# State space layer: pools allocated in another order, the next mixer's earliest weights split from inside it, and ScalarE's opening reordered

## The chip, the cores and the metric

The kernel runs on one core of one Trainium2 chip. The metric is the device time of one launch in microseconds (us), the median over several runs. A core has five engines with a queue of instructions each: PE (TensorE: matrix products and transposes), DVE (VectorE), ACT (ScalarE), POOL (GpSimd) and SP (SyncE, which here issues most of the transfers). An engine takes its instructions in the order that the compiler's scheduler wrote; semaphores tie the engines together.

## The reference

An encoder trunk of two layers over 512 tokens of 1024 numbers, in float32. Each layer is a token mixer and a channel mixer with a normalisation before and after:

```python
for layer in range(DEPTH):                       # DEPTH = 2
    hn = rms_norm(x, norm_mix_pre[layer])
    m = retention_na_mixer(hn, ...) if layer % 2 == 0 else ssd_mixer(hn, ...)
    x = x + rms_norm(m, norm_mix_post[layer])
    f = conv_geglu_ffn(rms_norm(x, norm_ffn_pre[layer]), ...)
    x = x + rms_norm(f, norm_ffn_post[layer])
```

Layer 0's mixer is retention beside neighbourhood attention. Layer 1's is a state space mixer: one projection gives gates z, inputs xs, keys B, queries C and step sizes; a depthwise convolution of width 5 and a silu follow; a scan runs in both directions in chunks of 128 tokens; `y * silu(z)` is normalised in four groups and projected back. The channel mixer projects to 2 x 2816 features, convolves over three tokens, takes `gelu(gate) * value` and projects back.

## The kernel before, in words

The program is four stages on one core: `mixer0` and `ffn` for layer 0, `mixer1` and `ffn` for layer 1, with x resident in SBUF as four tiles of 128 tokens, t0 to t3. Tokens that feed a product are normalised (`norm`: a sum of squares on ACT, `ssx`, tile junk; `r_x` by a power on POOL; `xs` in two halves on DVE), transposed by PE eight blocks at a time (`turn`, tile pt, L148), and split into a high part xh (an ACT cast, L86) and a low part xl (a DVE subtraction, L87). Products run in a reduced-precision float format, so each is three: high with high, high with low, low with high (`mm3`, L91 to L93).

Weights come from DRAM as 128 x 1024 float32 pieces, 512 KB each, into the tile wst, of which there are three; SP issues the loads in program order. `wunit` loads a piece and splits it in the same manner: an ACT cast to whi, a DVE subtraction to wlo. For some pieces the parts lie elsewhere: the third and fourth weight of an ffn are split into four half pieces, hh and hl.

A scheduler orders the instructions of each engine. It is told priorities (`high_priority(n)`), and follows dependences between tiles and those added by hand with `together`. Tiles come out of pools; a pool's place in memory depends on the order in which pools are opened, and a tile that reuses a place waits for the last user of it, so the order of pools is itself an input to the schedule.

`mixer1` handles four groups of eight heads. A table (`SLOTS`) lists in which order the steps of a group are written: `n` and `t` project the next weights (bf, cf, xf: key, query and input, each followed by ACT's first tap of the convolution, L693, and four DVE taps, L696), `h` makes a head's decay matrix (rows pb are broadcast from DRAM by a transfer that ACT issues, L751; eight ACT steps shift them, L762; a DVE copy masks them; ACT takes the exponential into `e`, L766; DVE multiplies), `i` and `p` do the products pi and py and end with y, N the silus (z, L702 and L705). Exponential and silu need different function tables, and ACT loads one (ACT_TABLE_LOAD) at each switch. The epilogue projects y back, tile by tile (m), adds it to x, which is reloaded from DRAM half by half (xd, L869), and normalises the sum (`ssm`, `r_m`, mg, x). `finish` runs these steps as they are listed in TAIL and LATE.

`ffn` begins with four projections (two features pieces, gate and value) over the first 256 tokens and then over the second 256, so that it can start before the last tokens are ready; between them E.flush() lets the last tiles' transposes in. In the products of this stage the first two weights are whi, wlo and the next two hh, hl.

At the program's start the four tiles of x are loaded, with the first three weights of `mixer0` between them, and each is normalised and turned.

## Time and profile before

| | us |
|---|---|
| median of three runs | 1422.65 |
| runs | 1420.84, 1422.65, 1425.30 |
| the profiled execution | 1422.91, its span 1421.1 |
| PE busy in the span | 1395.8 (98%) |
| DVE, ACT, POOL busy | 909.3, 710.6, 60.9 |
| PE's first transposes start | 8.17 |
| mixer1's first group of heads | from about 700 |
| start of the second ffn | about 1044 |

In the rows of the timeline the first number is the start in us from the start of the span, the second the busy time, then engine, line, operation, the tile written and those read; `x3` says how many follow on each other. In square brackets stands the idle time of the engine ahead of the row and the engine, tile and line that ended it. The profile's line numbers are those of the kernel before. A table of stretches gives, for each stretch, its length, the busy time of PE, PE's weight loads, DVE, ACT and POOL, the granted clock of PE as a share of full speed, the share of the transfer engines in use and GB/s.

### The profile page before, as it was taken

To read this page: it belongs to the slowest core of one execution; us is meant where nothing else is said; L and a number is where in the kernel's file an instruction comes from. 1 tells how busy PE (TensorE), PEld (TensorE's weight loads), DVE (VectorE), ACT (ScalarE), POOL (GpSimd) and SP (SyncE) were. 2 spreads that over 40 slices of the span, in tenths; PEclk is the share of its full clock that TensorE was granted. 3 is DMA by queue.
4 is the path that set the end of the run, shared out by engine and by line. 5 is a ranking of instruction groups with operands and counts; after the bars stand their busy time and mean duration, and the time that the engine had idled before them with its cause. 6 is when DMAs were issued, how large, how long until landed. Compare 5 with 4: busy or idle time off the path is not lost.

```text
span 1421.1 us, 17833 instructions
## 1 busy us (share of the span) xinstructions
PE 1395.8 (98%) x6838; PEld 1141.2 (80%) x6838; DVE 909.3 (64%) x1345; ACT 710.6 (50%) x1194; POOL 60.9 (4%) x66
## 2 busy tenths in 40 slices
PE   7999999999999999999999999999989999999998
PEld 6877777898888888888788788787878888888886
DVE  7368888765656652347878686997785665664232
ACT  5346666444444432324878787487344444443230
POOL 1010110100000000000000000010110000000000
PEclk9999999999999999999999999999999999999999
DMA  7443232233233322323566464363342233333231
GB/s 284 150 132 104 85 89 80 77 108 104 89 104 91 102 89 93 129 106 106 140 183 182 148 184 143 101 190 112 124 144 74 91 102 91 102 96 98 89 104 60
DMA packets 56437, 166.33 MB, mean 117 GB/s; under 512 B 6689, under 2 KB 7457, under 8 KB 56353
## 3 DMA queue, kind: packets, MB, share of 16 engines
q1 hardware_dynamic: 48464, 149.99, 33.2%
q10 hardware_dynamic: 7888, 15.21, 3.9%
q8 instruction: 54, 0.88, 0.3%
q14 instruction: 31, 0.25, 0.1%
HBM read 157.57 MB, written 5.51 MB: 115 GB/s over the span
## 4 chain that ended last, share of the span: by engine, by line
PE 89%; DVE 4%; ACT 3%; issue 2%; DMA 1%; POOL 0%; DVEq 0%; SPq 0%; POOLq 0%; ACTq 0%
PE mm L91 27%; PE mm L92 27%; PE mm L93 27%; PE pi L783 2%; PE py L803 1%; PE st L732 1%; PE y L459 1%; PE pt L148 1%; PE sc L443 1%; DVE wlo L87 1%; PE pt L676 0%; PE sc L444 0%; ACT whi L86 0%; DMA x<-in_x 0%; PE pt L511 0%
## 5 line engine op out<-in xcount | busy, mean ns | idle before, releaser
L91 PE MATMUL mm<-xh,whi 128*128 128x512 f32 (+1 forms) x1216 | 463.9, 382 | 0.4 <-ACT xh L86 0.2
L93 PE MATMUL mm<-xl,whi 128*128 128x512 f32 (+2 forms) x1216 | 463.3, 381 | 0.0
L92 PE MATMUL mm<-xh,wlo 128*128 128x512 f32 (+2 forms) x1216 | 462.1, 380 | 0.0
L87 DVE TENSOR_TENSOR wlo<-wst,whi 128x1024 fp32r<-128x1024 f32 (+1 forms) x208 | 254.8, 1226 | 135.0 <-ACT whi L86 131.7
L86 ACT CAST whi<-wst 128x1024 fp32r<-128x1024 f32 (+1 forms) x208 | 216.5, 1042 | 145.1 <-PE mm L92 123.4
L91 PEld LDWEIGHTS mm<-xh,whi 128*128 128x128 f32 x1216 | 228.3, 188 | 45.7 <-issue 2.3
L93 PEld LDWEIGHTS mm<-xl,whi 128*128 128x128 f32 (+1 forms) x1216 | 228.1, 188 | 44.1 <-issue 1.1
L92 PEld LDWEIGHTS mm<-xh,wlo 128*128 128x128 f32 (+1 forms) x1216 | 228.4, 188 | 42.4 <-issue 0.2
L237 DVE SCALAR_TENSOR_TENSOR cv<-mm,cwt,cv 128x511 f32<-128x511 f32 x88 | 66.0, 750 | 150.5 <-ACT cv L236 150.5
L236 ACT ACTIVATE cv<-mm,cwt 128x512 f32<-128x512 f32 x88 | 68.7, 780 | 128.0 <-PE mm L93 128.0
L91 PE MATMUL mm<-whi,hh 128*128 128x512 f32 x288 | 112.0, 389 | 0.0
L92 PE MATMUL mm<-whi,hl 128*128 128x512 f32 x288 | 112.0, 389 | 0.0
L93 PE MATMUL mm<-wlo,hh 128*128 128x512 f32 x288 | 112.0, 389 | 0.0
L762 ACT ACTIVATE pb<-pb,tok 128x128 f32<-128x128 f32 x256 | 81.3, 391 | 5.7 <-DMA pb<-pd 3.2
L86 ACT CAST hh<-cv 128x512 fp32r<-128x512 f32 x44 | 27.3, 621 | 103.3 <-DVE cv L245 103.3
L238 DVE SCALAR_TENSOR_TENSOR cv<-mm,cwt,cv 128x511 f32<-128x511 f32 x88 | 66.0, 750 | 3.0
L93 PEld LDWEIGHTS mm<-wlo,hh 128*128 128x128 f32 x288 | 54.1, 188 | 11.3
L91 PEld LDWEIGHTS mm<-whi,hh 128*128 128x128 f32 x288 | 54.1, 188 | 11.2
L92 PEld LDWEIGHTS mm<-whi,hl 128*128 128x128 f32 x288 | 54.1, 188 | 11.2
L696 DVE SCALAR_TENSOR_TENSOR xf<-mm,cwt,xf 128x511 f32<-128x511 f32 (+1 forms) x64 | 47.5, 744 | 8.1 <-ACT xf L693 7.8
L87 DVE TENSOR_TENSOR hl<-cv,hh 128x512 fp32r<-128x512 f32 x44 | 30.5, 693 | 28.9 <-ACT hh L86 28.9
L128 ACT ACTIVATE junk<-mm 128x512 bf16<-128x512 f32 x24 | 14.3, 596 | 68.7 <-PE mm L93 68.6
(250 smaller groups left out, 1877.1 us busy)
## 6 DMA issues: line engine op xcount, KB each, us to landing
wst<-in_f_up SPq DMA_DIRECT2D x88, 512.0 KB
wst<-in_f_down SPq DMA_DIRECT2D x44, 512.0 KB
wst<-in_c_fm SPq DMA_DIRECT2D x40, 512.0 KB
pb<-pd ACTq DMA_DIRECT2D x29, 512.0 KB
wst<-in_ab_fm SPq DMA_DIRECT2D x20, 512.0 KB
gain<-yd SPq DMA_DIRECT2D x32, 256.0 KB
wst<-in_c_out SPq DMA_DIRECT2D x16, 512.0 KB
gain<-in_norms SPq DMA_DIRECT2D x8, 512.0 KB
```

The costliest lines, as they stand in the source:

```text
L86: self.nc.scalar.copy(hi, src)
L87: self.nc.vector.tensor_tensor(lo, src, hi.bitcast(F32), op=ALU.subtract)
L91: mm(out, lh, rh, start=first, stop=False)
L92: mm(out, ll, rh, start=False, stop=False)
L93: mm(out, lh, rl, start=False, stop=last)
L128: self.nc.scalar.activation(self.junk[:, :w], src, AF.Square, scale=float(n) ** -0.5, accum_out=s)
L236: nc.scalar.activation(o, ps, AF.Identity, scale=w(1), bias=w(3))
L237: nc.vector.scalar_tensor_tensor(o[:, 1:], ps[:, :S - 1], w(0), o[:, 1:], op0=ALU.mult, op1=ALU.add)
L238: nc.vector.scalar_tensor_tensor(o[:, :S - 1], ps[:, 1:], w(2), o[:, :S - 1], op0=ALU.mult, op1=ALU.add)
L696: nc.vector.scalar_tensor_tensor(r[:, a], ps[:, b], wc(j), r[:, a], op0=ALU.mult, op1=ALU.add)
L762: nc.scalar.activation(pb[:, dr, c], pb[:, dr, c], AF.Identity, scale=1.0 - 2 * dr, bias=tok[:, 0, c, dr * H + h:dr * H + h + 1])
L783: nc.tensor.matmul(pi[:, c - 1 + dr], o["st"][dr, i][:, q * P:(q + 1) * P], o["t"][1][:, c * C:(c + 1) * C], start=True, stop=True)
```

## The change

It has three parts, and none changes what is computed. The instructions are the same but for one ACT instruction more.

In the opening, ACT gets a square of a single number ahead of everything else, which brings its table. The loads of `mixer0`'s first weights stay where they were, and their splits are written behind the turning of the tokens: a weight's cast is tied behind the second xh cast of tile t, and the square of t1 behind the first xh cast of t0.

In `mixer1` the pools ys and last are opened ahead of `three`, and the rows pb leave `three` for a pool of their own, hrows, with three buffers. The small tiles ss and rg go to another pool, a gap of 32 numbers and a smaller pad keep the addresses of others, and the epilogue's mg comes from `three` under the tag e, in place of z's place.

Between `mixer1` and the second `ffn`, `ahead` loads and splits the ffn's first two weights from inside `mixer1`, the second behind the last yh, and loads the third. In `ffn` the splits of the third and fourth weight (hh) are tied behind the last xh cast of t1, those of the fifth and sixth behind the last xh cast of t2 and t3.


```diff
@@ Env
-        pool("pad", 1).tile([P, 80], F32, name="pad")
+        pool("pad", 1).tile([P, 48], F32, name="pad")
...
-        self.late, self.xs = [], {}
-
-    def wunit(self, src, parts=None):
-
-
-        nc = self.nc
+        self.late, self.xs, self.turned = [], {}, {}
+
+    def wload(self, src):
+
         st = self.wst.tile([P, 1024], F32, name="wst")
-        nc.sync.dma_start(st, src)
+        self.nc.sync.dma_start(st, src)
+        return st
+
+    def wunit(self, src, parts=None, st=None, ahead=60, behind=None):
+        if st is None:
+            st = self.wload(src)
...
-            with self.tc.high_priority(60):
-                self.split(hi, lo, st)
+            with self.tc.high_priority(ahead) if ahead else nullcontext():
+                self.split(hi, lo, st, behind)
...
-    def split(self, hi, lo, src):
-
-        self.nc.scalar.copy(hi, src)
+    def split(self, hi, lo, src, behind=None):
+
+
+        first = self.nc.scalar.copy(hi, src)
         self.nc.vector.tensor_tensor(lo, src, hi.bitcast(F32), op=ALU.subtract)
+        if behind:
+            self.together([first], [behind])
+        return first
...
-    def norm(self, t, g_pre):
+    def norm(self, t, g_pre, behind=None):
 
         nc = self.nc
-        r = self.power("x", self.sumsq(self.xe[:, t, :], D, "ssx"))
+        r = self.power("x", self.sumsq(self.xe[:, t, :], D, "ssx", behind))
...
-                self.split(self.xh[o], self.xl[o], pt)
+                self.turned.setdefault(t, [None, None])[h] = self.split(self.xh[o], self.xl[o], pt)
@@ ffn
-def ffn(E, w_up, cw, w_down, g_post_row, done):
+def ffn(E, w_up, cw, w_down, g_post_row, done, w1=None):
...
-        nc.sync.dma_start(cwt, cw)
...
-        w0 = [[E.wunit(w_up[s, f], extra() if 2 * f + s >= 2 else None) for s in range(2)] for f in range(2)]
+        u0, u1, st = w1 or (E.wunit(w_up[0, 0]), E.wunit(w_up[1, 0]), None)
+
+        behind = E.turned[1][1] if w1 else None
+        w0 = [[u0, u1], [E.wunit(w_up[0, 1], extra(), st, behind=behind), E.wunit(w_up[1, 1], extra(), behind=behind)]]
+        nc.sync.dma_start(cwt, cw)
...
-                w = E.wunit(w_up[s, f])
+                w = E.wunit(w_up[s, f], behind=E.turned[2 + s][1] if w1 and f == 2 else None)
@@ mixer1
-def mixer1(E, w_dt, w_fm, cw, dtc, cols, mask, w_out, g_post_row, done):
+def mixer1(E, w_dt, w_fm, cw, dtc, cols, mask, w_out, g_post_row, done, ahead):
...
+        few.tile([P, 32], F32, name="gap")
         few.tile([P, 32], F32, name="pad")
...
-                pbs.append(three.tile([P, 2, NT, C], F32, name="pb", bufs=3))
+                pbs.append(hrows.tile([P, 2, NT, C], F32, name="pb"))
...
-            nc.scalar.activation(yh, y, AF.Identity, scale=col[:, 1, f:f + 1])
+            o["yh"] = nc.scalar.activation(yh, y, AF.Identity, scale=col[:, 1, f:f + 1])
...
-            o["ss"] = few.tile([P, NT], F32, name="ss", bufs=2)
+            o["ss"] = E.small.tile([P, NT], F32, name="ss", bufs=2)
...
-            o["r"] = few.tile([P, NT], F32, name="rg", bufs=2)
+            o["r"] = E.small.tile([P, NT], F32, name="rg", bufs=2)
...
-        three, ys, last = pool("m1e", 5), pool("m1y", 2), pool("m1f", 1)
+        ys, last, hrows, three = pool("m1y", 2), pool("m1f", 1), pool("m1p", 3), pool("m1e", 5)
...
-            E.post_half(st, t, n, m, g_post, None, four.tile([P, 512], F32, name="mg", tag="z"))
+            E.post_half(st, t, n, m, g_post, None, three.tile([P, 512], F32, name="mg", tag="e"))
...
+        ahead(gs[-1]["yh"])
         first = [out_mm(gs[-1], 0, ws[n]) for n in range(2)]
@@ trunk
-        w0 = []
+        ws, w0 = [], []
...
                 g0 = E.bcast(norms[0, 0])
+
+                nc.scalar.activation(E.junk[:, :1], E.mhalf, AF.Square)
             else:
-                w0.append(E.wunit(ab[0][0, len(w0)]))
+                ws.append(E.wload(ab[0][0, len(ws)]))
         for t in range(NT):
-            E.norm(t, g0)
+
+            E.norm(t, g0, E.turned[0][0] if t == 1 else None)
             E.turn(t, 0 if t else 100)
+            if t < len(ws):
+                w0.append(E.wunit(None, st=ws[t], ahead=0, behind=E.turned[t][1]))
...
-        mixer1(E, *ssd, norms[1, 1], then(norms[1, 2]))
-        ffn(E, *ffns[1], norms[1, 3], store)
+        w1 = []
+
+        def ahead(w):
+            up = ffns[1][0]
+            w1.extend((E.wunit(up[0, 0]), E.wunit(up[1, 0], behind=w), E.wload(up[0, 1])))
+
+        mixer1(E, *ssd, norms[1, 1], then(norms[1, 2]), ahead)
+        ffn(E, *ffns[1], norms[1, 3], store, w1)
```

The order on the engines moves more than these lines say. On ACT, in the first group of `mixer1`, before (whi_6056 is the cast of the weight for cf):

```order
L762 ACTIVATE pb_5493<-pb_5493,tok_5147 128x128 x8
L86 CAST whi_6056<-wst_6054 128x1024
L766 ACT_TABLE_LOAD
L766 ACTIVATE e_5783<-pb_5489 128x512
L766 ACTIVATE e_5865<-pb_5491 128x512
L751 DMA pb_5785<-pd_5149 128x2x512
L751 DMA pb_5867<-pd_5149 128x2x512
L702 ACT_TABLE_LOAD
L702 ACTIVATE z_5851<-mm_5826 128x512
L705 ACTIVATE z_5708<-mm_5683 128x512
L705 ACTIVATE z_5740<-mm_5715 128x512
L705 ACTIVATE z_5819<-mm_5794 128x512
```

and with the change (the same weight is whi_6061, bf_5942 is the first tap of the key convolution):

```order
L827 ACTIVATE sq_5886<-y_5763 128x512
L841 ACTIVATE yh_5888<-y_5763,col_5140 128x512
L780 ACTIVATE pb_5790<-pb_5790,tok_5149 128x128 x7
L780 ACTIVATE pb_5872<-pb_5872,tok_5149 128x128 x3
L784 ACT_TABLE_LOAD
L784 ACTIVATE e_5971<-pb_5790 128x512
L711 ACTIVATE bf_5942<-mm_5917,cwt_5136 128x512
L769 DMA pb_5973<-pd_5151 128x2x512
L780 ACTIVATE pb_5872<-pb_5872,tok_5149 128x128 x2
L93 CAST whi_6061<-wst_6059 128x1024
L780 ACTIVATE pb_5872<-pb_5872,tok_5149 128x128 x3
L93 CAST whi_6112<-wst_6110 128x1024
```

The cast of this weight stood ahead of the first exponentials; it now stands behind y's square, ten steps of pb, a table load, an exponential and bf.

On ACT, at the start of the second ffn, before (pt_8995 and pt_9002 are the transposes of tile t2; hh are the third and fourth weight, whi_9228 the sixth):

```order
L86 CAST xh_100<-pt_8995 128x4x128
L86 CAST xh_100<-pt_9002 128x4x128
L86 CAST whi_9228<-wst_9226 128x1024
L86 CAST hh_8923<-wst_8927 128x512
L86 CAST hh_8924<-wst_8927 128x512
L86 CAST hh_8933<-wst_8937 128x512
L86 CAST hh_8934<-wst_8937 128x512
L128 ACTIVATE junk_99,ssx_8874<-x_97 128x1025
```

and with the change (pt_8901 and pt_8908 are those of t1, pt_9001 and pt_9008 of t2; whi_9203 is the fifth weight; ssm1 is the last square of t3):

```order
L93 CAST xh_100<-pt_8901 128x4x128
L93 CAST xh_100<-pt_8908 128x4x128
L93 CAST hh_8930<-wst_8659 128x512
L93 CAST hh_8931<-wst_8659 128x512
L93 CAST hh_8938<-wst_8942 128x512
L93 CAST hh_8939<-wst_8942 128x512
L138 ACTIVATE junk_99,ssx_8825<-x_97 128x1025
L138 ACTIVATE junk_99,ssm0_8864<-m_8860 128x512
L93 CAST xh_100<-pt_9001 128x4x128
L93 CAST xh_100<-pt_9008 128x4x128
L93 CAST whi_9203<-wst_9201 128x1024
L138 ACTIVATE junk_99,ssm1_8884<-m_8880 128x512
```

The hh casts moved from behind t2's casts and a weight's to right behind t1's; a weight's cast now stands between t2's xh casts and the square ssm1 of t3.

On DVE at the same place, before (the last two x are tile t3's; wlo_9198 is the fifth weight's):

```order
L161 TENSOR_TENSOR mg_8844<-m_8841,gain_8608 128x512
L868 SCALAR_TENSOR_TENSOR m_8861<-mm_8848,rg_8674,x_97 128x512
L87 TENSOR_TENSOR wlo_9198<-wst_9195,whi_9197 128x1024
L139 SCALAR_TENSOR_TENSOR xs_8810<-x_97,r_x_8808,gain_8696 128x512
L139 SCALAR_TENSOR_TENSOR xs_8812<-x_97,r_x_8808,gain_8696 128x512
L114 TENSOR_SCALAR v_m_8867<-ssm0_8845,ssm1_8865 128x1
L161 TENSOR_TENSOR mg_8864<-m_8861,gain_8608 128x512
L185 SCALAR_TENSOR_TENSOR x_97<-mg_8844,r_m_8869,x_97 128x512
L185 SCALAR_TENSOR_TENSOR x_97<-mg_8864,r_m_8869,x_97 128x512
L87 TENSOR_TENSOR xl_101<-pt_8995,xh_100 128x4x128
```

and with the change (v_m is what POOL makes r_m of t3 from; x and xs are of t3):

```order
L886 SCALAR_TENSOR_TENSOR m_8880<-mm_8867,rg_8693,x_97 128x512
L94 TENSOR_TENSOR xl_101<-pt_9001,xh_100 128x4x128
L173 TENSOR_TENSOR mg_8883<-m_8880,gain_8613 128x512
L94 TENSOR_TENSOR xl_101<-pt_9008,xh_100 128x4x128
L124 TENSOR_SCALAR v_m_8886<-ssm0_8864,ssm1_8884 128x1
L94 TENSOR_TENSOR wlo_9204<-wst_9201,whi_9203 128x1024
L197 SCALAR_TENSOR_TENSOR x_97<-mg_8863,r_m_8888,x_97 128x512
L197 SCALAR_TENSOR_TENSOR x_97<-mg_8883,r_m_8888,x_97 128x512
L151 SCALAR_TENSOR_TENSOR xs_8897<-x_97,r_x_8895,gain_8715 128x512
L151 SCALAR_TENSOR_TENSOR xs_8899<-x_97,r_x_8895,gain_8715 128x512
```

The fifth weight's wlo stood ahead of t2's xs; it now stands between v_m and x of t3.

More of the change, by code (lines that the diff above doesn't have):

```diff
@@ L69, in wunit @@
             hi, lo = self.whi.tile([P, 1024], R32, name="whi"), self.wlo.tile([P, 1024], R32, name="wlo")
-            with self.tc.high_priority(60):
-                self.split(hi, lo, st)
+            with self.tc.high_priority(ahead) if ahead else nullcontext():
+                self.split(hi, lo, st, behind)
             return [(hi[:, c], lo[:, c]) for c in halves]
-        with self.tc.high_priority(60):
+        with self.tc.high_priority(ahead):
             for j, c in enumerate(halves):
-                self.split(parts[j], parts[j + 2], st[:, c])
+                self.split(parts[j], parts[j + 2], st[:, c], behind)
         return [(parts[j], parts[j + 2]) for j in range(2)]
@@ L122, in power, with sumsq @@
         return r
-    def sumsq(self, src, n, name):
+    def sumsq(self, src, n, name, behind=None):
         s = self.small.tile([P, 1], F32, name=name)
         w = src.shape[-1]
-        self.nc.scalar.activation(self.junk[:, :w], src, AF.Square, scale=float(n) ** -0.5, accum_out=s)
+        m = self.nc.scalar.activation(self.junk[:, :w], src, AF.Square, scale=float(n) ** -0.5, accum_out=s)
+        if behind:
+            self.together([m], [behind])
         return s
-    def norm(self, t, g_pre):
+    def norm(self, t, g_pre, behind=None):
         nc = self.nc
-        r = self.power("x", self.sumsq(self.xe[:, t, :], D, "ssx"))
+        r = self.power("x", self.sumsq(self.xe[:, t, :], D, "ssx", behind))
         self.xs[t] = []
```

## The prediction, as it was made before the run

> **What bounds the kernel now.** I read the page's busy times first, then the waits of PE, then the clock and the queues at each long wait. In the waits the columns are total us, times, longest.
>
> ```profile
> PE 1395.8 (98%) x6838; PEld 1141.2 (80%) x6838; DVE 909.3 (64%) x1345; ACT 710.6 (50%) x1194; POOL 60.9 (4%) x66
> PE pt L148 <- DVE xs L139: 9.1, 4, 8.2
> PE mm L91 <- ACT hh L86: 3.9, 2, 3.2
> PE pi L783 <- DVE state L740: 0.5, 1, 0.5
> ```
>
> PE is the bound: 25.3 us of the span are idle, and only PE's waits can be won back. The edits can reach the opening (8.2), the start of the second ffn (3.9 and a slow clock behind it), and the state space mixer, where PE hardly waits and any new wait is a loss. PE's program has the same products before and after.
>
> The start of the second ffn, PE, then the clock (PEclk is the seventh figure: the share of full speed) and the queues of ACT and SP:
>
> ```profile
> 1050.91 1.29 PE L148 MATMUL pt<-head,xs 128*128 128x128 f32 x8
> 1055.42 0.38 PE L91 MATMUL mm<-xh,hh 128*128 128x256 f32 x1 [3.21 <-ACT hh L86]
> 1056.46 0.58 PE L91 MATMUL mm<-xh,hh 128*128 128x256 f32 x1 [0.66 <-ACT hh L86]
> 1062.06 1.29 PE L148 MATMUL pt<-head,xs 128*128 128x128 f32 x8
> 1065.93 0.28 PE L91 MATMUL mm<-xh,whi 128*128 128x256 f32 x1
> 1066.30 0.28 PE L91 MATMUL mm<-xh,whi 128*128 128x256 f32 x1
> ...
> 1054.00:1056.00 2.00, 0.38 (x1) 0.19 (x1) 2.00 (x3) 2.00 (x4) 0.00 (x0) 0.94 0.71 244
> 1056.00:1062.00 6.00, 5.54 (x24) 5.30 (x25) 4.15 (x7) 1.98 (x4) 1.08 (x1) 0.50 0.69 219
> 1062.00:1064.00 2.00, 2.00 (x17) 2.00 (x16) 0.43 (x1) 1.05 (x2) 0.00 (x0) 0.85 0.32 129
> ...
> 1043.89 1.25 ACT L86 CAST xh<-pt 128x512 fp32r<-128x512 f32 x2 [0.71 <-PE pt L148]
> 1051.58 1.25 ACT L86 CAST xh<-pt 128x512 fp32r<-128x512 f32 x2 [1.64 <-PE pt L148]
> 1053.80 1.04 ACT L86 CAST whi<-wst 128x1024 fp32r<-128x1024 f32 x1 [0.97 <-DMA wst<-in_f_up]
> 1054.75 2.17 ACT L86 CAST hh<-wst 128x512 fp32r<-128x512 f32 x4
> 1056.83 1.06 ACT L128 ACTIVATE junk<-x 128x1025 bf16<-128x1025 f32 x1
> ...
> 1028.84 19.95 SPq L869 DMA_DIRECT2D x<-xd  x8
> 1049.64 0.33 SPq L66 DMA_DIRECT2D wst<-in_f_up  x1
> ```
>
> PE needs hh at about 1052.2 and gets it at 1055.42. ACT was held by the cast at 1053.80, whose weight was asked for at 1049.64, behind eight reloads of x. Then the clock halves: at half speed it ran for 0.24 us of 1054-56, all 6.0 of 1056-62 and 0.60 of 1062-64, 6.8 us in all, of which PE was busy some 6.1 and lost half, 3.0. The pass over the second half of the tokens starts at 1065.93. Products of 256 columns follow each other by (1066.30 - 1065.93)/3 = 0.12 us.
>
> **The change, start of the ffn.** The four hh casts now stand right behind t1's xh casts; of the casts to whi, the fifth weight's stands behind t2's xh, the sixth's, which held them, behind t3's. In the clock of before t1's xh casts end at 1045.1, so ACT has hh done by about 1047.4 (four in 2.17) and DVE hl before 1052. PE's 3.2 and 0.7 us of waiting go. The first pass loses a little: wlo of the second weight now stands in the epilogue's DVE chain, on which PE's transposes already wait; it costs 0 to 1.2 us, and I take 0.45. So the t2 transposes start at 1051.1, and 48 products run from 1052.0 to 1052.0 + 48 x 0.12 = 1057.75.
>
> What is late next is token tile t3:
>
> ```profile
> 1049.22 0.63 ACT L128 ACTIVATE junk<-m 128x512 bf16<-128x512 f32 x1
> 1048.51 1.47 POOL L121 TENSOR_TENSOR r_x<-ssx,head 128x1 f32<-128x1 f32 x1 [4.02 <-ACT junk L128]
> 1041.75 0.55 POOL L121 TENSOR_TENSOR r_x<-ssx,head 128x1 f32<-128x1 f32 x1 [2.77 <-ACT junk L128]
> 1048.37 1.22 DVE L87 TENSOR_TENSOR wlo<-wst,whi 128x1024 fp32r<-128x1024 f32 x1
> 1052.58 1.41 DVE L185 SCALAR_TENSOR_TENSOR x<-mg,r_m,x 128x512 f32<-128x512 f32 x2 [0.43 <-POOL r_m L121]
> 1059.17 1.41 DVE L139 SCALAR_TENSOR_TENSOR xs<-x,r_x,gain 128x512 f32<-128x512 f32 x2 [0.44 <-POOL r_x L121]
> ```
>
> On ACT, t3's last square (ssm1) now stands behind the t2 casts (1051.75 + 1.25) and the fifth weight's cast (1.04): it runs 1054.0 to 1054.8. DVE then has v_m at 1054.9 and the fifth weight's wlo, 1.2 us, ahead of x. POOL's r_m runs beside this wlo, where a 0.55 us step took 1.47 and ended 0.4 after it (1048.51 against 1048.37): 1056.6. x adds 1.4 (1058.0), its square 1.25, r_x and a gap 0.65 (1059.9), the first half of xs 0.75. The transposes of t3 start at 1060.65, so PE waits again, 2.9 us. The next pass needs xh of t3 (0.55 transposes, 0.75 for the cast): 1061.95 against 1065.93, a gain of **3.9 us** if the clock stays up. Were r_m not slowed, x would still wait for wlo to end: 0.4 less. The eighth reload of x goes out behind two weight loads and could land near 1057; that is no earlier a bound than 1056.6.
>
> The Trainium skill ("TensorE: Matmul & The Clock Gate", Part 1) gives a free-running window of about 3.4 us, of which one idle one halves the clock; the slow stretch of 6.8 us here is two such windows. Its Part 4 says that transposes don't count as busy in the same way; the hole between products would then be 1057.75 to 1061.95 and can hold a window, which speaks against this change's gain; counted as work, they leave 2.9 us. That is the second rival below.
>
> **The change, opening.** Rows of ACT and PE:
>
> ```profile
> 4.25 1.28 ACT L128 ACT_TABLE_LOAD   x1 [4.25 <-DMA x<-in_x]
> 7.85 1.06 ACT L128 ACTIVATE junk<-x 128x1025 bf16<-128x1025 f32 x1 [1.16 <-DMA x<-in_x]
> 8.17 1.97 PE L148 MATMUL pt<-head,xs 128*128 128x128 f32 x8 [8.17 <-DVE xs L139]
> 9.06 1.04 ACT L86 CAST whi<-wst 128x1024 fp32r<-128x1024 f32 x1
> 11.24 0.77 PE L91 MATMUL mm<-whi,xh 128*128 128x512 f32 x1
> ```
>
> The dummy square puts the 1.28 us table load ahead of x's landing at 4.25, so t0's transposes start 1.28 earlier, at 6.9. But t1 lands at 7.85 all the same, and the first weight cast, at 9.06 before, now stands behind three squares and two xh casts, near 11: the first product comes about 1.2 later. After that fewer transposes interleave. Placing ACT's rows one behind the other I have PE two 512-column products ahead at 22 us, 0.45 us (an estimate). From the table load alone the bound is -1.28; from the later first product, partly made good, +0.5. I take **-0.45**.
>
> **The change, the mixer's middle.** With pb in a pool of its own and `e` in another region, the scheduler has moved more than the diff says. In the first group the cast whi of the cf weight stood at 713.87; now it stands behind y's square, pb's, a table load, e and bf, and its wlo behind bf's four convolution steps on DVE.
>
> ```profile
> 713.87 1.05 ACT L86 CAST whi<-wst 128x1024 fp32r<-128x1024 f32 x1 [1.77 <-PE mm L93]
> 721.40 1.28 ACT L766 ACT_TABLE_LOAD   x1
> 722.70 0.64 ACT L766 ACTIVATE e<-pb 128x512 f32<-128x512 f32 x1
> 724.66 0.71 ACT L823 ACTIVATE yh<-y,col 128x512 fp32r<-128x512 f32 x1
> 727.36 0.78 ACT L693 ACTIVATE bf<-mm,cwt 128x512 f32<-128x512 f32 x1 [1.99 <-PE mm L93]
> 728.03 3.31 ACT L762 ACTIVATE pb<-pb,tok 128x128 f32<-128x128 f32 x11
> 728.17 2.32 DVE L696 SCALAR_TENSOR_TENSOR bf<-mm,cwt,bf 128x511 f32<-128x511 f32 x3 [1.70 <-ACT bf L693]
> 732.60 0.39 PE L91 MATMUL mm<-xh,whi 128*128 128x512 f32 x1
> ...
> 696.58 5.82 DMA pb<-pd
> ```
>
> From the end of yh (725.3): ten pb at 0.30 (3.31/11) 728.3, table 1.28, e 0.64, bf 0.78: bf ends at 731.0 instead of 728.0. DVE's four steps at 0.77 end at 734.1, wlo at 735.3. PE wants it for its second product of that weight, 732.60 + 0.24 = 732.8 (512 columns, twice 0.12): **2.5 us** of waiting. Bounds: if yh ends at 724.8, 2.0. If the ACT queue is held by the first pb step, which now stands ahead of the z's: its load goes out near 714.2, and the row of 5.82 us puts it at 720; two us more there make the wait 4.5. Below nothing it cannot be; nothing is the fourth rival. In turn pi's 0.5 us wait has five products ahead of it now: **-0.5**. Other weights of this mixer keep their place within 2 us of queue work; the rest of it I take at nothing, covered by ACT's half-empty queue.
>
> **The sum.** -0.45 + 2.5 - 0.5 - 3.9 = -2.35. The profiled run took 1422.91 around a span of 1421.1, 0.26 above the median of 1422.65; against the median the forecast is **1420.3 us**, and with the bounds of its terms 1418.9 to 1421.8.
>
> **The rivals.**
>
> 1. The forecast: the wait moves from hh to t3's transposes, and a smaller one opens at the cf weight. Chance 0.38.
> 2. As before, but the clock halves again at the t3 wait. For it: it fell behind 3.2 us of idling at 1055; against it: 2.9 is shorter and no lone product follows. The slow stretch of before cost 3.0; half of it would cost 1.5; I take 2.2: 1422.5. Chance 0.20.
> 3. t3 is not late: the DVE chain is shorter than I place it, PE waits nowhere, and 2.9 + 0.75 more are won: 1416.6. Against it stand ssm1 behind two casts and wlo ahead of x. Chance 0.10.
> 4. The cf weight doesn't hold PE, because ACT gets through y's square and the pb's sooner than in before: 1420.3 - 2.5 = 1417.8. Against it: bf is tied to the products' end and everything behind it to bf. Chance 0.15.
> 5. Slower: the pb load lands late and holds the whole ACT queue at the first group; PE idles 4.5 us at the cf weight, longer than the 3.2 after which the clock fell in before, and loses the same 3.0 to it. -0.45 - 0.5 + 4.5 + 3.0 - 3.9 = +2.65: 1425.3. It decides from a pb step that starts after 720.5. Chance 0.17.
>
> **How the numbers follow.** About 0.3%, 4.3 us, is what a measurement of this kernel can tell from no change. Under 1418.4 lie the third, two thirds of the fourth and a tail of the first: 0.28. Over 1426.9 lies half of the fifth: 0.09. The rest, 0.63, is within. The range 1416.2 to 1426.0 leaves out half of the third and the upper part of the fifth.
>
> **What would show it.** In the waits of PE: `mm <- ACT hh` gone; `pt <- DVE xs` with a new wait near 3 us in the 1050s; a new `mm <- DVE wlo` of 2 to 3 us near 733; the first xs at 6.1. In the clock row: 1.00 through the ffn's start, or else the second rival. The forecast is wrong if the wait at t3 is under 1 us, or if PE stands over 4 us anywhere in the mixer.

## The result, and the profile after

The changed kernel takes 1424.38 us (median of 20 runs, 1423.01 to 1428.98) where the kernel before takes 1421.85 (20 runs beside them, 1420.79 to 1425.30): ratio 1.0018, with a 95% interval of 1.0011 to 1.0025. A second comparison gave 1424.30 against 1422.70, ratio 1.0013 [1.0004, 1.0023]. So the change costs 1.6 to 2.5 us of 1422. The time lies inside the stated range, but a gain of 2.35 us had been forecast (1420.3), so the sign was wrong.

The profiled execution of the changed kernel took 1423.01 us, its span 1421.1: the same span as the one profiled before. Both traces are single executions, the one before's 1.06 above its kernel's median, the other 1.4 below. What each stage gained or lost is read from the traces; what lies between traces and medians comes up again below.

In the busy times and the waits of PE (total us, times, longest), the changed kernel:

```profile
PE 1393.6 (98%) x6838; PEld 1140.1 (80%) x6838; DVE 909.4 (64%) x1345; ACT 711.1 (50%) x1195; POOL 62.3 (4%) x66
PE pt L160 <- DVE xs L151: 14.3, 5, 7.4
PE mm L102 <- DVE wlo L94: 1.7, 1, 1.7
```

The wait for hh is gone. Transposes wait 5.2 us more than before (14.3 against 9.1) and a wait for a weight's low part is new, as forecast. PE idles 27.5 us of the span (1421.1 - 1393.6) against 25.3.

The opening, timelines of ACT, DVE and PE of the changed kernel:

```profile
4.17 1.06 ACT L138 ACTIVATE junk<-x 128x1025 bf16<-128x1025 f32 x1 [1.94 <-DMA x<-in_x]
9.16 1.06 ACT L138 ACTIVATE junk<-x 128x1025 bf16<-128x1025 f32 x1
11.74 1.03 ACT L93 CAST whi<-wst 128x1024 fp32r<-128x1024 f32 x1
...
6.59 1.42 DVE L151 SCALAR_TENSOR_TENSOR xs<-x,r_x,gain 128x512 f32<-128x512 f32 x2 [5.19 <-DMA gain<-in_norms]
...
7.40 1.97 PE L160 MATMUL pt<-head,xs 128*128 128x128 f32 x8 [7.40 <-DVE xs L151]
11.79 2.38 PE L160 MATMUL pt<-head,xs 128*128 128x128 f32 x8 [2.42 <-DVE xs L151]
```

and t1's transposes in the trace of before:

```profile
10.47 1.11 PE L148 MATMUL pt<-head,xs 128*128 128x128 f32 x4 [0.34 <-DVE xs L139]
```

t0's square starts 1.37 us earlier than before (4.17 against 5.54), but its xs starts only 0.77 earlier, because it now waits for the transfer of the gain. t1's square starts at 9.16, behind t0's first xh cast, where it had started at 7.85 when x landed; so t1's transposes come at 11.79 and not at 10.47. The first product starts at 13.81 where it had started at 11.24.

The first group of `mixer1`, ACT, DVE and PE:

```profile
724.79 3.03 ACT L780 ACTIVATE pb<-pb,tok 128x128 f32<-128x128 f32 x10
729.66 0.76 ACT L711 ACTIVATE bf<-mm,cwt 128x512 f32<-128x512 f32 x1
730.91 1.04 ACT L93 CAST whi<-wst 128x1024 fp32r<-128x1024 f32 x1
...
730.46 3.10 DVE L714 SCALAR_TENSOR_TENSOR bf<-mm,cwt,bf 128x511 f32<-128x511 f32 x4
733.48 1.21 DVE L94 TENSOR_TENSOR wlo<-wst,whi 128x1024 fp32r<-128x1024 f32 x1
...
734.75 0.50 PE L102 MATMUL mm<-xh,wlo 128*128 128x512 f32 x1 [1.65 <-DVE wlo L94]
```

The cf weight is late by the chain that was forecast: ten pb steps, bf, four convolution steps, wlo.

The epilogue, DVE and PE:

```profile
1029.33 0.75 DVE L886 SCALAR_TENSOR_TENSOR m<-mm,rg,x 128x512 f32<-128x512 f32 x1
1030.00 1.22 DVE L94 TENSOR_TENSOR wlo<-wst,whi 128x1024 fp32r<-128x1024 f32 x1
1031.73 0.75 DVE L886 SCALAR_TENSOR_TENSOR m<-mm,rg,x 128x512 f32<-128x512 f32 x1
...
1040.15 0.63 PE L160 MATMUL pt<-head,xs 128*128 128x128 f32 x4 [0.94 <-DVE xs L151]
```

and the same transposes in the trace of before:

```profile
1037.11 0.63 PE L148 MATMUL pt<-head,xs 128*128 128x128 f32 x4 [0.39 <-DVE xs L139]
```

The second ffn weight's wlo stands between t0's two m, and an mg behind it: the second m starts 2.40 us after the first, where before it followed after 0.76 (1028.07 and 1028.83). t0's transposes wait 0.94 us where they waited 0.39.

The start of the second ffn: what token tile t3 waits for, then PE, then the table of stretches (the seventh figure is the granted clock):

```profile
1054.99 0.74 DVE L886 SCALAR_TENSOR_TENSOR m<-mm,rg,x 128x512 f32<-128x512 f32 x1
1055.76 0.33 SPq L887 DMA_DIRECT2D x<-xd  x1
1056.36 0.62 ACT L138 ACTIVATE junk<-m 128x512 bf16<-128x512 f32 x1
1057.57 1.22 DVE L94 TENSOR_TENSOR wlo<-wst,whi 128x1024 fp32r<-128x1024 f32 x1
1057.73 1.45 POOL L131 TENSOR_TENSOR r_m<-v_m,head 128x1 f32<-128x1 f32 x1 [5.32 <-DVE v_m L124]
1062.53 1.41 DVE L151 SCALAR_TENSOR_TENSOR xs<-x,r_x,gain 128x512 f32<-128x512 f32 x2 [1.90 <-POOL r_x L131]
1063.43 1.94 PE L160 MATMUL pt<-head,xs 128*128 128x128 f32 x8 [2.87 <-DVE xs L151]
```

```profile
1062.00:1064.00 2.00, 0.57 (x3) 0.60 (x4) 1.41 (x2) 0.00 (x0) 0.49 (x1) 0.81 0.01 4
1064.00:1066.00 2.00, 2.00 (x10) 1.78 (x9) 0.69 (x1) 1.17 (x2) 0.00 (x0) 0.50 0.03 8
1066.00:1068.00 2.00, 2.00 (x16) 2.00 (x16) 1.59 (x2) 1.05 (x1) 0.00 (x0) 0.83 0.00 0
```

t3's transposes wait 2.87 us, against a forecast of 2.9. The clock halves at the end of that wait, at 1063.26, for 3.4 us (0.76 of the first two, all of the second, 0.68 of the third), where it had been at half speed for 6.8 before.

Set beside each other, the start of one and the same PE instruction in two traces shows where time goes. The table gives after minus before, in us, at eight places that are named by their time in the trace of before; the second row is a second trace of the changed kernel (span 1421.3), from the last experiment. From 1066 to 1074.6 the changed kernel runs the same products in another order, a few of the third and fourth weight ahead of their place; 1075 is the first place behind that.

| | 88 | 713 (pi) | 746 | 1030 | 1037 (t0's transposes) | 1051 (t2's) | 1075 | 1412 |
|---|---|---|---|---|---|---|---|---|
| the change | +0.97 | +0.10 | +2.10 | +2.03 | +3.04 | +2.75 | 0.00 | 0.00 |
| the change, again | +2.09 | +1.11 | +3.05 | +3.07 | +4.35 | +4.06 | +0.21 | +0.21 |

Up to 88 us the change loses 1 to 2 us (1.1 of the second trace's is a longer wait for DVE's rk, 1.6 us for 0.5), pi gives 0.47 back, the cf weight takes 1.9 to 2.0, the epilogue 1.0 to 1.3, and the start of the ffn (from t2's transposes to 1075) returns 2.75 to 3.85. All of the gain is spent before it is made.

### The profile page after: what moved, and what is told of

Its sections match the earlier page's. It is cut to its first block, busy times and chain, and to the rows that moved or that the text cites. A ratio compares the mean times of both kernels' runs of the same rounds, so it can differ in the third digit from the quotient of the medians.

```text
span 1421.1 us, 17839 instructions
## 1 busy us (share of the span) xinstructions
PE 1393.6 (98%) x6838; PEld 1140.1 (80%) x6838; DVE 909.4 (64%) x1345; ACT 711.1 (50%) x1195; POOL 62.3 (4%) x66
## 4 chain that ended last, share of the span: by engine, by line
PE 90%; ACT 4%; DVE 3%; issue 1%; DMA 1%; POOL 1%; DVEq 0%; POOLq 0%; SPq 0%; ACTq 0%
PE mm L101 27%; PE mm L102 27%; PE mm L103 27%; PE pi L801 1%; PE st L750 1%; PE py L821 1%; PE pt L160 1%; PE y L475 1%; PE pt L694 1%; PE sc L459 1%; PE sc L460 0%; ACT junk L138 0%; PE pt L527 0%; PE y L537 0%; PE sc L510 0%
## 5 line engine op out<-in xcount | busy, mean ns | idle before, releaser
L138 ACT ACTIVATE junk<-mm 128x512 bf16<-128x512 f32 x24 | 14.3, 596 | 68.4 <-PE mm L103 68.3
```

The lines of the kernel that those rows point to most:

```text
L138: m = self.nc.scalar.activation(self.junk[:, :w], src, AF.Square, scale=float(n) ** -0.5, accum_out=s)
```

## Experiments

All were timed in five rounds against the kernel before, those of one table group on one chip.

| kernel | median, us | ratio to before, 95% interval |
|---|---|---|
| opening only | 1424.05 | 1.0004 [0.9995, 1.0013] |
| pools only | 1424.40 | 1.0012 [1.0002, 1.0022] |
| change, fifth weight later | 1423.29 | 0.9999 [0.9990, 1.0009] |
| change, a first-group weight early | 1422.56 | 0.9998 [0.9988, 1.0008] |
| | | |
| change without the pools | 1422.22 | 1.0001 [0.9991, 1.0011] |
| change, fifth weight later and reload earlier | 1420.46 | 0.9990 [0.9981, 0.9999] |
| change, cf weight early | 1423.52 | 1.0010 [1.0001, 1.0019] |
| together | 1419.20 | 0.9979 [0.9970, 0.9988] |
| | | |
| together, second weight untied | 1417.88 | 0.9964 [0.9951, 0.9976] |
| together, table early | 1419.15 | 0.9976 [0.9963, 0.9989] |
| together, new opening without t1's tie | 1419.24 | 0.9978 [0.9969, 0.9987] |
| | | |
| the change again | 1424.30 | 1.0013 [1.0004, 1.0023] |

**Opening only.** The kernel before with the third edit alone:

```diff
+                nc.scalar.activation(E.junk[:, :1], E.mhalf, AF.Square)
...
-            E.norm(t, g0)
+            E.norm(t, g0, E.turned[0][0] if t == 1 else None)
+            if t < len(ws):
+                w0.append(E.wunit(None, st=ws[t], ahead=0, behind=E.turned[t][1]))
```

> The kernel before with the new opening alone (table load early, first weights' casts behind the tokens' xh casts). Ledger theory (the two traces laid over each other at fixed places): PE is 0.7 us late from the first attention scores on, so 1422.6 against 1421.9 of before, and xs of t1 makes PE wait 2.4 us near 11.8. Rival (my forecast of the opening): 0.45 us faster, 1421.4, and the loss lies elsewhere.

Measured: 1.0004, an interval that holds no change and a loss of 1.8 us. In the trace t1's transposes start 1.35 us later than in the trace of before, and at 88 us PE stands at +1.23. The hh wait is as before (3.1 us, longest).

**Pools only.** The kernel before with the order of the pools and nothing of the other two parts:

```diff
-        three, ys, last = pool("m1e", 5), pool("m1y", 2), pool("m1f", 1)
+        ys, last, hrows, three = pool("m1y", 2), pool("m1f", 1), pool("m1p", 3), pool("m1e", 5)
```

> The kernel before with the new order of pools alone. Ledger theory: in the first group pi's wait of 0.5 us goes and the cf weight's wlo makes PE wait 1.7 to 2.0 us near 734; the start of the ffn keeps its hh wait of 3.2 us: +1.4 us, 1423.3. Rival (the cast is late only together with the other parts, or the wait is made good later in the mixer): 1421.9.

Measured: 1.0012, slower by 0.3 to 3.1 us. The loss in the groups of heads is here (PE goes from +1.15 at 703 us to +3.76 at 746, with waits of 1.0 us for wlo, 0.9 for ACT's z and 0.5 for xs), and so is the gain at the ffn's start: no wait for hh is left, and t3's transposes wait in its place. PE's timeline of this kernel:

```profile
1066.12 1.29 PE L160 MATMUL pt<-head,xs 128*128 128x128 f32 x8 [3.05 <-DVE xs L151]
```

So the pools alone move the hh splits. This bears on the diff: the ties of the hh casts behind t1's xh casts are not what brings them forward.

**The change without the pools**, the other side of the same question. The edit undoes every line on pools (m1e, hrows, the place of mg, ss, rg and the pads).

> Opening and ffn start as in the change, pools of the state space layer as before. Theory: the order of the pools is what lets the hh weights be split early, and it is also what costs 1 to 2 us in the first groups of heads. Then here the hh wait is back (2.5 to 3.5 us at 1055), the clock halves behind it, there is no wait of a first-group product on the cf weight (mm <- DVE wlo under 0.3), and the ratio to before is 1.000 to 1.001. Rival: the ties by hand and the early split suffice; the hh wait is under 1 us, and with no cost in the groups of heads the ratio is 0.996 to 0.998.

Measured: 1.0001. The hh wait is back, and its row on ACT says what the casts stood for: not the weight, but t3's x, on DVE:

```profile
1060.80 1.66 ACT L93 CAST hh<-wst 128x512 fp32r<-128x512 f32 x3 [1.12 <-DVE x L197]
...
1061.47 0.39 PE L101 MATMUL mm<-xh,hh 128*128 128x256 f32 x1 [2.46 <-ACT hh L93]
```

That x is the last reader of an mg in the old place, so the tile hh seems to take a place in memory that is free only then; with the new order of pools it is free earlier. That this is a matter of the place is read from the releaser and from the two runs, which differ in nothing but places. No product waited for the cf weight here, so that cost belongs to the pools as well. At t0's transposes PE lost 1.22 us (+6.35 at 1030, +7.57 at 1037), so the epilogue's loss does not need the new order of pools. The pools alone lose some there too, 0.5 us up to t1's transposes (+4.12 at 1030, +4.58 at 1043), so the early split of the second ffn weight is not shown to be the whole of it.

**Fifth weight later.** The change, with the fifth ffn weight's split tied behind t3's xh casts like the sixth's:

```diff
-                w = E.wunit(w_up[s, f], behind=E.turned[2 + s][1] if w1 and f == 2 else None)
+                w = E.wunit(w_up[s, f], behind=E.turned[3][1] if w1 and f == 2 else None)
```

> The changed kernel, with one edit: the fifth weight of the ffn is split behind t3's last xh cast instead of t2's. Theory (t3's chain is held on ACT by this weight's cast, 1.04 us, and on DVE by its wlo, 1.2 us, beside which POOL's r_m takes 1.5 instead of 0.5): PE's wait at t3's transposes falls from 2.9 us to under 0.7, the clock stays at 1.00, and the time falls by 2.5 (wait) to 4.1 us (with the slow clock): 1420.3 to 1421.9. Rival (t3 is late because of the reload of x or of the epilogue's own chain): the wait stays near 2.9 and the time at 1424.4.

Measured: 0.9999, by the ratios 2.0 to 2.7 us under the change. SP's queue, DVE and PE:

```profile
1057.70 0.33 SPq L887 DMA_DIRECT2D x<-xd  x1
...
1060.93 0.75 DVE L197 SCALAR_TENSOR_TENSOR x<-mg,r_m,x 128x512 f32<-128x512 f32 x1 [0.54 <-DMA x<-xd]
...
1064.48 1.75 PE L160 MATMUL pt<-head,xs 128*128 128x128 f32 x8 [1.95 <-DVE xs L151]
```

With wlo out of the way r_m takes 0.54 us and not 1.45, and the wait falls by 0.92, not to nothing. The next thing that is late is the eighth reload of x: it goes out once the second m of t3 is through, and that m stands on DVE behind the four hl. The clock fell again.

**Fifth weight later and reload earlier.** As the last one, and the four hh splits lose their raised priority, which puts t3's second m ahead of the four hl:

```diff
-        w0 = [[u0, u1], [E.wunit(w_up[0, 1], extra(), st, behind=behind), E.wunit(w_up[1, 1], extra(), behind=behind)]]
+        w0 = [[u0, u1], [E.wunit(w_up[0, 1], extra(), st, ahead=0 if w1 else 60, behind=behind),
+                         E.wunit(w_up[1, 1], extra(), ahead=0 if w1 else 60, behind=behind)]]
```

> The change with the fifth ffn weight split behind t3's transposes (as in the experiment before) and the four hh splits without their raised priority, so that on DVE the second m of t3, which the eighth reload of x waits for, stands ahead of the four hl and not behind. Theory: with the fifth weight out of the way, t3 is late by that m: the reload goes out about 3 us sooner, the wait of t3's transposes falls from 1.95 to under 0.6 us, the clock stays at 1.00 from 1060 to 1070, and the ratio to before falls from 0.9999 to 0.997 to 0.9985. Rival one: the chain of t3 on ACT, POOL and DVE is what is late, whatever the reload; the wait stays over 1.2 us, the clock falls again, ratio 0.9995 to 1.0005. Rival two: the hl come late in turn, PE waits over 1 us for hh or hl near 1054, ratio 0.9995 to 1.001.

Measured: 0.9990 [0.9981, 0.9999], a little above the 0.997 to 0.9985 expected. DVE and PE:

```profile
1051.32 0.74 DVE L886 SCALAR_TENSOR_TENSOR m<-mm,rg,x 128x512 f32<-128x512 f32 x1
...
1057.74 0.39 PE L102 MATMUL mm<-xh,hl 128*128 128x256 f32 x1 [0.63 <-DVE hl L94]
1060.23 0.63 PE L160 MATMUL pt<-head,xs 128*128 128x128 f32 x4 [0.31 <-DVE xs L151]
```

and a row of its stretches:

```profile
1064.00:1066.00 2.00, 2.00 (x19) 2.00 (x18) 1.61 (x2) 0.17 (x1) 0.00 (x0) 1.00 0.27 86
```

t3's wait goes from 1.95 to 0.31 us, an hl is late by 0.63 in turn, and the clock stays up. From t2's transposes to 1075 us PE gains 5.9 us on the kernel before, where the change gained 2.75 to 3.85 and the last kernel 3.6. The four kernels that follow with this edit gain 5.9 there as well. By time the step from 0.9999 to 0.9990 is not separated; in the traces it is 2.3 us.

**A first-group weight early.** This one missed its aim: the priority raised was that of a gate's weight (the ninth of the group), not that of the cf weight that its expectation speaks of.

```diff
-                w = E.wunit(w_fm[g, i])
+                w = E.wunit(w_fm[g, i], ahead=600 if (g, i) == (0, 8) else 60)
```

> The changed kernel, with one edit: the split of the cf weight of the second group gets a higher priority (600 in place of 60), which puts its cast 11 us of ACT's work earlier. Theory: PE's wait of 1.7 us on this wlo goes, and what was behind it is not late: 2.0 us less, 1422.4. Rival (the wait only moves to py or to the next weights, since ACT and DVE have as much to do as before): 1424.4.

The scheduler moved the cf weight's cast ahead all the same (it starts at 717.46), the wait for wlo was gone, and a wait of 1.0 us for DVE's xs was new. At 0.9998 it stands 2 to 3 us under the change, but since it moved more than one thing it says little about the one weight.

**cf weight early**, the edit as it was meant:

```diff
+                w = E.wunit(w_fm[g, i], ahead=600 if (g, i) == (1, 1) else 60)
```

> The change with one priority raised, that of the cf weight in the first group of heads; its cast goes back ahead of the pb steps that it was put behind. Theory: this weight alone is what the first group lost; its wait (1.7 us) goes, PE's clock of events from 746 us to 1030 stands 1.5 to 2 us earlier against the change, and the ratio to before falls from 1.0018 to 1.0003 to 1.0008; the wait at t3 (2.9 us) and the half clock behind it stay. Rival: ACT and DVE are full there, so another wait (z, xf or the state) takes its place; under 0.7 us is won and the ratio is 1.0012 or more.

Measured: 1.0010, between the two theories, and not separated from the change's 1.0018 or 1.0013. The trace is clearer: the cast goes back to 715.24, no product waits for wlo, and from 703 to 1030 us PE loses 0.34 us on before (+1.84 to +2.18) where the change lost 1.46 and 1.49. So the weight's new place costs 1.1 us net: the change pays 2.0 for it and has 0.47 back at pi, the early cast pays 0.34 in a wait for a gate.

**Together.** The opening as before; pools and ffn start as in the change with the three edits (cf weight early, fifth weight later, hh without raised priority).

> The opening as before; pools and ffn start as in the change, with the cf weight of the first group raised, the fifth ffn weight's split behind t3 and the hh splits without raised priority. Theory (three separate losses that add): 1.0018 less 0.0013 for the cf weight, less 0.0019 for the fifth weight, less 0.0015 to 0.002 for the reload and the clock, and 0 to 0.0004 less for the opening: 0.9965 to 0.998, faster than both kernels. Rival (they share one slack, or the epilogue's 1 us and the run-to-run scatter of the opening eat it): 0.999 to 1.0005.

Measured: 0.9979 [0.9970, 0.9988], 1419.20 us: faster than both kernels, at the upper end of the expected 0.9965 to 0.998. That fits losses that add up, at the weak end of the sum.

**Second weight untied.** Together, and:

```diff
-            w1.extend((E.wunit(up[0, 0]), E.wunit(up[1, 0], behind=w), E.wload(up[0, 1])))
+            w1.extend((E.wunit(up[0, 0]), E.wunit(up[1, 0]), E.wload(up[0, 1])))
```

> The kernel of the experiment before (all together) with one tie less: the split of the second ffn weight is not tied behind the last yh, so that on DVE its wlo (1.22 us) stands nine rows earlier, ahead of the last group's yl, and no longer between the first and the second m of t0. Theory: that wlo is what the epilogue lost in the change; the wait of t0's transposes falls by 0.9 to 1.2 us (from 0.94 to below 0.4 us), and the ratio to before falls from 0.9979 to 0.997 to 0.9975. Rival: ahead of yl it holds yl and so the last products as long as it held m; PE's events at t0's transposes stay where they were within 0.3 us, ratio 0.9975 to 0.9985.

Measured: 0.9964 [0.9951, 0.9976], 1417.88 us, the best of all. PE's timeline, first of this kernel:

```profile
1038.31 1.29 PE L160 MATMUL pt<-head,xs 128*128 128x128 f32 x8 [0.67 <-DVE xs L151]
```

and of the kernel together:

```profile
1039.12 0.63 PE L160 MATMUL pt<-head,xs 128*128 128x128 f32 x4 [0.87 <-DVE xs L151]
```

The expectation was half met: t0's wait fell by 0.2 us, and with t1's (0.70 to 0.24) the epilogue lost 0.4 us less from 1030 on. As the rival had it, part of that is paid ahead of it: between 1000 and 1030 us this kernel loses 0.24 us (+0.45 to +0.69) where the kernel together loses nothing. The tie accounts for less than half of the epilogue's loss. Of the rest the traces show that the mg still stands between t0's two m, which start 1.38 us apart here and 0.76 in the kernel before; moving it was not tried. The times of the two kernels are not separated.

**Table early.** Together, with ACT's table loaded early and the rest of the old opening.

> All together, but with the new opening's first half: ACT's table is loaded early, while the casts of the first weights and t1's square stand as before the change. Theory: t0's xs waits for the gain's transfer, which lands near 6.5 us whatever ACT does, so t0's transposes start near 7.4 (8.1 without) and t1's near 10.4, as before; the first product is no later than before; at 88 us the events stand 0 to 0.7 us earlier than in the kernel with the old opening, as far as the moment at which the products reach full rate lets one see it; ratio 0.997 to 0.9982. Rival: the early table costs as the change's opening did (+1 us at 88 us); ratio 0.9985 or more.

Measured: 0.9976, as the kernel together. t0's transposes start at 7.28 and t1's at 10.38, as the theory has it: 0.8 us of the first tile, nothing of the second. At 88 us PE stands at +1.21, as in the pools-only kernel (+1.25), whose products reached full rate at the same moment, 16.7 us, without the early table. The early table is worth nothing here.

**New opening without t1's tie.** Together with the change's opening, and:

```diff
-            E.norm(t, g0, E.turned[0][0] if t == 1 else None)
+            E.norm(t, g0)
```

> All together with the change's opening, less one tie: t1's square does not wait for t0's first xh cast. The weights' splits stay behind the tokens. Theory: the tie alone moved t1's transposes from 10.5 to 11.8 us; without it they start near 10.4, the products reach full rate about 1.2 us earlier, and the opening costs nothing: events at 88 us at 0 to +0.8 against the profiled run of before, ratio 0.997 to 0.9985. Rival: it is the late first weight that costs; the transposes come early, the first product still near 13.8 us, and the events at 88 us stand at +1 to +2, ratio 0.9985 to 0.9995.

Measured: 0.9978. ACT and PE:

```profile
7.82 1.06 ACT L138 ACTIVATE junk<-x 128x1025 bf16<-128x1025 f32 x1 [2.47 <-DMA x<-in_x]
...
10.45 1.97 PE L160 MATMUL pt<-head,xs 128*128 128x128 f32 x8 [1.07 <-DVE xs L151]
13.79 0.78 PE L101 MATMUL mm<-whi,xh 128*128 128x512 f32 x1
```

Both theories hold a part. t1's square starts when x lands and its transposes come at 10.45, so the tie is what had moved them. The first product is still at 13.8, as the rival had it, and the products reached full rate no sooner (17.5 us). At 88 us PE stands at +0.96, between the two; kernels with the tie and a moment as late as that (17.4 and 17.8 us) stood at +3.11, of which 1.1 is a wait for rk that the last experiment tells of, and +2.04; so at a like moment the tie is worth about 1.0 us. Time does not tell these openings apart.

**The change again**, for a second trace.

> The changed kernel once more, for a second trace: the first one's execution (1423.01 us) is the shortest of twenty, the median is 1424.38. Theory: what the first trace had better than the median is the moment at which the first products reach full rate (15.3 us, the earliest of the seven traces with this opening; the others 15.9 to 17.8). Then this trace has that moment after 15.8, events at 88 us at +1.2 to +2.0 against the profiled run of before (+0.97 in the first), the waits of the cf weight (1.0 to 1.7), of t0's transposes (0.9 to 1.5) and of t3's (2.8 to 3.1) as before with one slow stretch of the clock of 3.4 us behind the last, and a span of 1421.8 to 1423.5; ratio 1.001 to 1.0025. Rival: the opening is as in the first trace and the span longer by something else, another wait or a second slow stretch.

Measured: 1.0013. The theory fell: full rate came by 15.5 us, as in the first trace. The two traces differ in a wait of 1.6 us for DVE's rk near 90 us (0.5 in the first, 1.6 also in the change without the pools), and the clock, which did not fall at t3. PE and two stretches:

```profile
1064.75 1.29 PE L160 MATMUL pt<-head,xs 128*128 128x128 f32 x8 [2.87 <-DVE xs L151]
```

```profile
1064.00:1066.00 2.00, 1.22 (x8) 0.84 (x8) 1.26 (x2) 0.58 (x1) 0.00 (x0) 1.00 0.01 2
1066.00:1068.00 2.00, 1.99 (x17) 1.95 (x17) 1.58 (x3) 1.64 (x2) 0.00 (x0) 1.00 0.03 8
```

## Why the prediction was wrong

**The wait that goes, and the one that comes: right.** The hh wait went, and t3's transposes wait 2.87 us for the forecast 2.9. Without a slow clock the stage gains 3.85 us (second trace) for the forecast 3.9. The chain was the one described: from t2's transposes to the end of r_m it took 5.5 us, as forecast. The eighth reload of x, which the forecast took for no earlier a bound than r_m, is nearly as late: it is issued at 1055.76, since it waits for the second m of t3, and that m stands behind the four hl on DVE. So both bound: without wlo the wait is still 1.95, and with m ahead of the hl it is 0.31.

**The clock: the second rival came in.** "The clock halves again at the t3 wait" had 0.20. It happened in three of the five traces that have this wait at 2.9 to 3.1 us: in the change and in the two kernels with one first-group weight early, and not in the change's second trace nor with the pools only. The change and those two gained 2.75, 2.4 and 2.4 us from 1051 to 1075, the other two 3.85 and 3.8: one fall costs some 1.3 us, for the 2.2 that the rival was given. The traces understate how common it is. The mean granted clock of a whole run reads 0.998 or less in all 20 runs of the change and in 9 of the 11 of the second comparison, where the second trace, without the fall, reads 0.999; the five kernels without this wait read 0.999 or 1.000 in 41 of 43 runs. So by this figure the fall belongs to nearly every run of the change.

The forecast argued that 2.9 us of idling is shorter than the 3.2 after which the clock had fallen. The length of a wait does not decide it: a wait of 1.95 us (fifth weight later) brought a fall, and waits of 2.87 and 3.05 did not. Nor does the whole hole between products, transposes included: 4.63 us in the change (1060.56 to 1065.19) and 4.62 before (1050.80 to 1055.42) ended in a fall, and so did 3.48 (fifth weight later), but 4.36 (pools only) did not, and one of 4.18 did (cf weight early) and another did not (the second trace). What sorts them is how much of one step of a fixed grid of 3.413 us the idling takes, of which the last section tells: PE was busy for 21% of that step in the change's first trace and for 59% in the second. The Trainium skill ("TensorE: Matmul & The Clock Gate", Part 1) has a free-running window of about 3.4 us; the traces agree. Its Part 4 says that transposes do not count as busy in the same way; here a count without them does not sort the traces (22% busy with products in two steps that ended in no fall, 35% in one that did), and a count with them does (59% and 43%).

**The opening: the step that failed most.** The term was -0.45, with bounds to +0.5; at 88 us the traces of the change say +1.0 and +2.1, or +1.0 for both without the longer wait for rk. One trace of before is a narrow base for this, since the moment of full rate moves it. The four traces with the old opening stand at 0.0 to +1.25 themselves, 0.5 in the mean; the eight with the change's stand at +0.95 to +2.04, 1.5 in the mean, when the 1.1 us of rk is taken off the two that have it. So the opening costs about 1.0 us where 0.45 of gain was forecast. Three sentences of it were wrong. "t0's transposes start 1.28 earlier, at 6.9": they started 0.77 earlier, since xs also needs the gain, whose transfer ends near 6.5. "t1 lands at 7.85 all the same": it does, but the square of t1 was tied behind t0's first xh cast, and that tie moves t1's transposes by 1.3 us. The kernel without the tie shows it. "the first product comes about 1.2 later": it came 2.6 later (13.81 for 11.24), with the tie or without. The gain of two products by 22 us, an estimate, was not there. How much of this reaches the median is open: alone the opening's ratio is 1.0004 [0.9995, 1.0013].

**The cf weight and pi: right.** 2.5 us were forecast for the cf weight in PE's course, 2.0 and 1.9 came (its wait is 1.65 and 1.4); pi gave 0.47 for the forecast 0.5. Rival 5, the late pb load, didn't come: the pb step that was to decide it started at 719.02, before 720.5.

**The epilogue: mis-sized.** 0.45 was taken, inside the 3.9, from bounds of 0 to 1.2; it measured 1.0 and 1.3 at t0's transposes, 0.7 and 1.0 at t2's. The forecast looked at the wlo alone; an mg came between t0's two m as well, and the second m came 1.6 us later behind the first than before.

**The sum.** With what the two traces measured in place of each term (the loss up to 88 us +1.5, the mean of the two; cf 1.95 for 2.5; pi -0.47; the epilogue +1.15; the stage of the ffn -3.3, the mean) the forecast of -2.35 becomes 1.5 + 1.95 - 0.47 + 1.15 - 3.3 = +0.8. The two traces end at 0.0 and +0.2, because a further 0.4 is regained between 88 and 703 us and 0.3 in the epilogue behind t0. The bounds stated with the forecast, 1418.9 to 1421.8, were also narrower than those of its terms added up: taken with the 0.4 of r_m these reach from 1418.1 to 1422.0, and to 1424.0 with the late pb load.

The medians differ by 2.5 and 1.6. The two traced executions of the change, 1423.01 and 1423.21, are among the shortest of their runs, 1.4 and 1.1 under the medians, and the traced one of before lies 1.06 above. The second trace lacks the fall of the clock that nearly all runs have; with its 1.3 it comes to 1424.5, about the median. The first has the fall and lacks 1.1 of the wait for rk; with it it would come to 1424.1. That most runs have both was not traced, and stays open.

## What to carry to other kernels

When a wait is taken away, look for the next late input, and count how long PE idles in any 3.4 us around it, not only whether the wait got shorter: here a wait of 1.95 us still brought the clock down, and only two more moves (the fifth weight's split, and the m that lets the last reload go) closed the gap and kept the clock. An order of pools is an edit of the schedule: it freed the place that the early splits needed, and in another stage put a weight's cast 17 us later (730.91 for 713.87), so its price is found by reading the order of every stage that uses the pools. Before an instruction is moved ahead, look for its second input (here the gain), and before one is tied to another, for when the operand that it really needs lands.

## What the runs showed of the hardware

**The first products run at half rate up to a moment that changes from run to run.** In the opening, products of 512 columns follow each other by 0.43 us and then, from one product to the next, by 0.23. PE's timeline of the change, and of the kernel with a first-group weight early (the same opening):

```profile
15.10 0.60 PE L102 MATMUL mm<-whi,xl 128*128 128x512 f32 x1
15.54 0.39 PE L101 MATMUL mm<-whi,xh 128*128 128x512 f32 x1
15.77 0.40 PE L103 MATMUL mm<-wlo,xh 128*128 128x512 f32 x1
```

```profile
16.80 0.63 PE L102 MATMUL mm<-whi,xl 128*128 128x512 f32 x1
17.23 0.63 PE L103 MATMUL mm<-wlo,xh 128*128 128x512 f32 x1
17.66 0.49 PE L102 MATMUL mm<-whi,xl 128*128 128x512 f32 x1
```

```profile
15.00:17.00 2.00, 2.00 (x7) 1.61 (x6) 1.85 (x4) 2.00 (x4) 1.15 (x1) 1.00 0.98 322
```

The last row is the stretch of that kernel from 15 to 17 us: the granted clock reads 1.00 there although the products are at half rate, so in the opening the rate is read from the products' spacing and not from that column: the trace's clock record, the list of changes from which the column is made, has its first entry at 17.87 us, and the column counts what lies ahead of it as full. The moment was 14.4 to 16.7 us in four traces with the old opening (14.7 in that of before) and 15.3 to 17.8 in eight with the change's. Each microsecond of it is worth about half a microsecond at 88 us (0.03, 0.00, 0.63 and 1.25 at 14.4, 14.7, 15.6 and 16.7 in the old opening), which is a good part of what single executions of one kernel differ by.

**The clock changes on a grid of 3.413 us, and fell where PE was busy for less than about half of one step.** The clock record of each of the fourteen traces has its changes whole multiples of 3.413 us apart: before at 14.69, 1055.76 and 1062.58 us (305 and 2 steps), in the change at 15.37, 1063.26 and 1066.67 (307 and 1). Where the grid begins differs from one execution to the next. PE's busy time, transposes included, was counted in every step from the first entry to 1412 us. Seven steps were busy for under half, 10 to 43%, all at the ffn's start, and each ended in a fall. Four were busy for 50 to 53%: one ended in a fall (the change without the pools, at 92.7 us, behind its wait for rk), three did not. None above that did. So the same hole can cost the clock in one execution and not in the next: of nine holes between products of 3.3 to 4.6 us at the ffn's start seven were followed by half speed.

**POOL's r_m** took 1.45 us beside DVE's wlo and 0.54 where that wlo had been moved away, the same instruction on the same tile.
